# Second mixer: attention pieces written between the channel tiles of the projections, scores in two-bank PSUM pairs

## The chip, the cores and the metric

One core of a Trainium2 chip runs the whole program. The metric is the device time of one execution in microseconds (us). The engines are TensorE (PE, with its weight loads PEld shown apart), VectorE (DVE), ScalarE (ACT), GpSimd (POOL, used here only to issue DMAs and to clear buffers) and SyncE (SP, which issues the weight loads from memory).

## The reference

A two-layer trunk over 384 tokens (256 latent ones, columns 0 to 255, and 128 context ones, columns 256 to 383), model width 1024, all in float32. Each layer is a feed-forward block, a mixer and a second feed-forward block. The change is in the second layer's mixer:

```python
def gqa_mixer(h, w_in, g_q, g_k, w_out, ctx):
    B, S, _ = h.shape
    q, k, v = jnp.split(h @ w_in, [MIX_C, MIX_C + GQA_KV_HEADS * GQA_HEAD_DIM], axis=-1)
    q = rms_norm(q.reshape(B, S, GQA_HEADS, GQA_HEAD_DIM), g_q)
    k = rms_norm(k.reshape(B, S, GQA_KV_HEADS, GQA_HEAD_DIM), g_k)
    ...                                   # rotary positions and 128 cached keys for the latent tokens
    o = block_attention(...)              # softmax(q k * 64 ** -0.5) v, 16 heads of 64, 4 of keys and values
    return o.reshape(B, S, MIX_C) @ w_out, (k, v)
...
x = x + gm * out
```

Latent tokens see 128 cached and 256 latent keys, context tokens their own 128. The first layer's mixer (eight heads, another projection, and a convolution beside it) shares the attention code, and so part of the change.

## The kernel before, in words

Activations are held channels by tokens. Every projection is done in three matmuls per channel tile (`mm3`): weights and activations are split into a high part and a remainder, and lo x hi, hi x lo and hi x hi are summed in PSUM. One "channel tile" k of a unit is the 128 input channels k for two output tiles of 128, so six matmuls of 384 or 386 columns. The activations' parts are `Hh`, `Hl` (mixer input) and `MXh`, `MXl` (attention output, 8 tiles of 128 channels, one for each pair of heads).

`stream` takes a list of steps. For each step it issues the weight splits for this step and the next, then the step before's `post` (what reads its PSUM result), then this step's matmuls. Weights come by DMA on SP's queue into three buffers `raw`. A split writes 1024 columns at a time into one of four pairs of buffers: `whi` by a cast on ACT (L205), and `wlo` either by a subtraction on DVE (L210), or, where a step has `add=True`, by a negated copy on ACT (L207) and a DMA on POOL's queue that adds the raw weights onto it (L208). Only the first mixer uses `add=True`.

The instructions are not run in the order written. A planner goes through them by that order, lets ready ones pass those that wait, and fixes each engine's sequence before the run. At run time each engine keeps to its sequence, so an instruction that is late holds what stands behind it.

The second mixer is `mixer_c`. Its input projection has six units (k and v in 0 and 1, q in 2 to 5), 48 matmuls each. A unit's `post` scales its two tiles, and for q adds the rotary part (L605 to L620, L1103). `head_sums4` sums squares over the head dimension and takes the reciprocal root, for four q tiles at a time; its result multiplies the scores (`sc`, `nsc`, L1113). Attention works by groups of two heads:

- `scores` (L644): three products a head into two PSUM banks a head, so four banks of `pmm`, which has four;
- `softmax` (L659 to L668): maximum on DVE, exponential and its sum on ACT, reciprocal and scaling on DVE, one head after the other;
- `pv`: seven transposes a head (L682, L686), copied to SBUF by ACT (L684) and DVE (L688), then the products with the values (L694), split into `MXh` and `MXl` (L610, L611).

The scores and the softmax of group 0 are written behind unit 4, the scores of group 1 ahead of unit 5, and the rest of group 0 behind it. Then comes the attention of groups 1 to 7, with nothing else written beside it, and then the output projection, four units of 48 matmuls, each with a `post` (`resid`, L464): it adds the gated result to the residual `X` (L467), makes the next block's `Hh` and `Hl` (L397, L399) and sums squares (L409, L410).

PSUM has eight banks: four one-bank buffers for `pmm`, two for `ptr`, two for `pax`.

Of the kernel before, what the change touches and what calls it, by code (L numbers as in the profile page):

```python
# [6 lines left out]
F32 = mybir.dt.float32  # L7
# [26 lines left out]

NLEAD = ND + 1
# [19 lines left out]
SH1, SC1, G1, SHM, SCM, GM, SH2, SC2, G2 = range(9)  # L55
# [4 lines left out]
def pair_col(i, k):  # L60

    return (k // 4 * 8 + i * 4 + k % 4) * P
# [18 lines left out]
class Trunk:  # L81
    def __init__(self, nc, tc, a):
        self.nc, self.tc, self.a = nc, tc, a
        self.mods = {}
        self.early = []
# [365 lines left out]
    def rsqrt(self, out, src, scale, v=None, w=None):  # L451
# [7 lines left out]
        for _ in range(3):  # L459
            ve.tensor_tensor(out=w, in0=out, in1=out, op=ALU.mult)  # L460
            ve.scalar_tensor_tensor(out=w, in0=w, scalar=-0.5, in1=v, op0=ALU.mult, op1=ALU.mult)  # L461
            ve.scalar_tensor_tensor(out=out, in0=w, scalar=1.5, in1=out, op0=ALU.add, op1=ALU.mult)  # L462

    def resid(self, d, ps, gate, nxt):  # L464
        nc = self.nc
        for s0, s1, c in SEG:
            nc.vector.scalar_tensor_tensor(  # L467
                out=self.X[:, d, s0:s1], in0=ps[:, s0:s1], scalar=gate[:, d, c:c + 1],
                in1=self.X[:, d, s0:s1], op0=ALU.mult, op1=ALU.add)
# [151 lines left out]

    def attention(self, heads, pairs, pool=None):

        nc = self.nc
        S = {}
        room = []
# [7 lines left out]
            return room[n // 3][:, n % 3 * 7 * P:(n % 3 + 1) * 7 * P]  # L634

        def scores(hs):
            for h in hs:
                S[h] = (self.ps_mm(), self.ps_mm())
            for dst, c0, cols, q0 in ((0, 0, slice(0, T), 0), (0, T, slice(T, 512), TL), (1, 0, slice(0, T), P)):
                for h in hs:  # L640
                    qT, kT, rows = heads[h][:3]
                    kw = {"tile_position": (rows.start, 0)} if pairs else {}
                    n = cols.stop - cols.start
                    nc.tensor.matmul(S[h][dst][:, c0:c0 + n], lhsT=qT[rows, q0:q0 + P], rhs=kT[rows, cols],  # L644
                                     start=True, stop=True, **kw)

        Pm = {}

        def softmax(hs):

            st = {h: (self.tb("mx", 3, 4), self.tb("sm", 3, 4), scratch(0, h)) for h in hs}
            part = lambda h, i: (S[h][0][:, 0:T], S[h][1][:, 0:T], S[h][0][:, T:512])[i]
            off = (0, T, 2 * T, 7 * P)
            for ids in ((0, 2), (1,)):
                for h in hs:
                    mx, sm, pr = st[h]
                    sc, nsc = heads[h][4], heads[h][5]
                    for i in ids:
                        nc.vector.reduce_max(out=mx[:, i:i + 1], in_=part(h, i), axis=AX.X)  # L659
                    c = slice(ids[0], 3, 2)  # L660
                    nc.vector.tensor_tensor(out=mx[:, c], in0=mx[:, c], in1=nsc[:, c], op=ALU.mult)
                    for i in ids:
                        nc.scalar.activation(pr[:, off[i]:off[i + 1]], part(h, i), AF.Exp, scale=sc[:, i:i + 1],
                                             bias=mx[:, i:i + 1], accum_out=sm[:, i:i + 1])
                    nc.vector.reciprocal(sm[:, c], sm[:, c])
                    for i in ids:
                        p, r = pr[:, off[i]:off[i + 1]], sm[:, i:i + 1]
                        nc.vector.tensor_scalar(out=p, in0=p, scalar1=r, scalar2=None, op0=ALU.mult)  # L668
            for h in hs:
                S.pop(h)  # L670
                Pm[h] = st[h][2]

        def pv(hs, MXh, MXl, ps=None):
            pts = []
            for h in hs:
                pr = Pm.pop(h)
                pt = scratch(1, h).rearrange("p (a b) -> p a b", b=P)
                pts.append(pt)
                ta, tb = (ps or (self.ps_ax if h == hs[1] else self.ps_tr))(), (ps or self.ps_tr)()
                for kt in range(2):  # L680
                    for qb in range(2):
                        nc.tensor.transpose(ta[:, (2 * kt + qb) * P:(2 * kt + qb + 1) * P],  # L682
                                            pr[:, qb * T + kt * P:qb * T + kt * P + P], self.ident)
                nc.scalar.copy(pt[:, 0:4, :], ta.rearrange("p (a b) -> p a b", b=P))  # L684
                for i, o in enumerate((2 * P, T + 2 * P, 2 * T)):
                    nc.tensor.transpose(tb[:, i * P:i * P + P], pr[:, o:o + P], self.ident)  # L686
                copy = nc.vector.tensor_copy if pool else nc.scalar.copy
                copy(pt[:, 4:7, :], tb[:, 0:3 * P].rearrange("p (a b) -> p a b", b=P))  # L688
# [9 lines left out]

        groups = [list(range(i, i + 2)) for i in range(0, len(heads), 2)]

        def first():
            scores(groups[0])
            softmax(groups[0])

        def ahead(i):
            if i + 1 < len(groups):
                scores(groups[i + 1])

        def group(i, MXh, MXl, ps=None):
            pv(groups[i], MXh, MXl, ps)  # L710
            if i + 1 < len(groups):
                softmax(groups[i + 1])
            self.pop_bg(BG2)

        def rest(MXh, MXl, i0=0):
            for i in range(i0, len(groups)):
                ahead(i)
                group(i, MXh, MXl)

        return first, rest, ahead, group  # L720

    def out_steps(self, w, MXh, MXl, gate, nxt):
        steps = []
# [47 lines left out]
    def mixer_a(self, l, nxt):  # L771
        nc, a, tc = self.nc, self.a, self.tc
        with tc.tile_pool(name="ma", bufs=1, reuse_waits="tile") as mp:
# [7 lines left out]
            with tc.tile_pool(name="map", bufs=1, reuse_waits="tile") as pp:  # L781
# [147 lines left out]
                heads = []  # L929
                for h in range(8):  # L930
                    V = lambda kt, h=h: Vt[:, kt, 64 * h:64 * h + 64]
                    heads.append((qT[h], kT[h], slice(0, P), V, rs, nrs, h // 2, h % 2))
                first, rest, _, _ = self.attention(heads, False)
                w = a["wia"]

                def bg(s):
# [71 lines left out]
    def mixer_c(self, l, nxt):  # L1008
        nc, a, tc = self.nc, self.a, self.tc
        with tc.tile_pool(name="mc", bufs=1, reuse_waits="tile") as mp:  # L1010
# [87 lines left out]
            def p_q(i):  # L1098
                def f(ps):
# [8 lines left out]
                    if i % 4 == 3:  # L1108
                        four = qq[-4:]

                        def sums():
                            r = head_sums4(four)
                            nc.vector.tensor_scalar(out=sc[i // 4], in0=r, scalar1=0.125, scalar2=None, op0=ALU.mult)  # L1113
                            nc.vector.tensor_scalar(out=nsc[i // 4], in0=r, scalar1=-0.125, scalar2=None, op0=ALU.mult)
                        (self.mid if i == 3 else self.later).append(sums)
                return f

            posts = [p_k(0), p_k(1), p_v(0), p_v(1)] + [p_q(i) for i in range(8)]
            heads = []
            for i in range(8):  # L1120
                for h in range(2):
                    kv = 2 * (i % 2) + h
                    V = lambda kt, kv=kv: Vt[:, kt, 64 * kv:64 * kv + 64]
                    norms = [x[i // 4][:, 2 * (i % 4) + h:24:8] for x in (sc, nsc)]
                    heads.append((qT[i], kT[i % 2], slice(64 * h, 64 * h + 64), V, *norms, i, h))
            first, rest, ahead, group = self.attention(heads, True, mp)
            steps = []
            for u in range(6):
                steps.append(self.in_unit(a["wic"][u], posts[2 * u:2 * u + 2]))
# [165 lines left out]
```

## Time and profile before

| | |
|---|---|
| Median of 3 runs | 1481.43 us (1478.88 to 1482.4) |
| The profiled execution | 1478.81 us; its span, first to last instruction, 1477.0 us |
| Granted TensorE clock, mean | 0.992 of full speed |
| PE, PEld | 98% and 95% of the span busy |
| DVE, ACT | 80% and 45% |
| Second mixer, unit 4 to the last output matmul | 1075.51 to 1185.09, 109.58 us |

A row of the timeline has the start, the length, the engine, the line of the kernel, the operation, what it writes and reads, how many instructions the row stands for, and in brackets the idle time before it with what ended it. Lengths of neighbouring matmuls overlap, since PE starts one before the last has drained; the step from start to start is what each costs in a row. A group of the page has the number of instructions, the busy time, the mean duration in ns, and the idle time ahead.

### The profile page before, as it was taken

Reading aid. Unit: us, or ns where it says so; the run is one execution under the profiler, and the core shown is the slowest. Engines: PE = TensorE matmul, PEld = TensorE weight load, DVE = VectorE, ACT = ScalarE, POOL = GpSimd, SP = SyncE. Lnnn points to the kernel's source line nnn. Section 1 sums busy time; section 2 is a strip of 40 time slices with the busy share of each in tenths; the row PEclk is TensorE's granted clock in tenths of the full one; section 3 lists DMA queues with packets and bytes.
Section 4 is the critical chain, followed back from the end, with each engine's and each line's share of the span. In section 5 each row is a group of like instructions: output and inputs, shape, how many; then the busy total and the mean of one; then the engine's idle time right before and its main releaser. Section 6 shows DMA issues by size and latency. Waiting matters only on the chain. (4 is left out here: it accounts for less than half of the span.)

```text
span 1477.0 us, 21867 instructions
## 1 busy us (share of the span) xinstructions
PE 1442.5 (98%) x8278; PEld 1397.7 (95%) x8278; DVE 1178.5 (80%) x2515; ACT 665.3 (45%) x1171; POOL 26.0 (2%) x36
## 2 busy tenths in 40 slices
PE   6999999999989999999999999999999999999997
PEld 5999999999869999999999999999975999999997
DVE  6999999949996999999969997544799688555433
ACT  4443343368666433343344334333476544333332
POOL 0000000021100000000000000000000000000000
PEclk8999999999999999999999999999999999999999
DMA  9655657699646566656565663334420264332341
GB/s 365 239 218 213 243 179 265 213 234 222 149 109 165 233 230 226 228 193 240 197 254 200 217 232 113 100 136 145 137 85 30 65 234 158 124 134 88 118 132 49
DMA packets 44633, 262.53 MB, mean 178 GB/s; under 512 B 4944, under 2 KB 6768, under 8 KB 21232
## 3 DMA queue, kind: packets, MB, share of 16 engines
q1 hardware_dynamic: 38160, 245.04, 46.0%
q0 software_dynamic: 4032, 14.16, 5.2%
q10 hardware_dynamic: 2336, 1.94, 0.4%
q8 instruction: 65, 1.06, 0.3%
q14 instruction: 40, 0.33, 0.1%
HBM read 244.98 MB, written 1.98 MB: 167 GB/s over the span
## 5 line engine op out<-in xcount | busy, mean ns | idle before, releaser
L205 ACT CAST whi<-raw 128x1024 fp32r<-128x1024 f32 (+1 forms) x348 | 329.5, 948 | 583.2 <-PE ps_mm L274 508.5
L272 PE MATMUL ps_mm<-Hh,wlo 128*128 128x386 f32 x1568 | 533.2, 341 | 5.7 <-DVE wlo L210 4.1
L273 PE MATMUL ps_mm<-Hl,whi 128*128 128x386 f32 x1568 | 532.4, 340 | 1.1 <-DVE Hl L399 1.1
L274 PE MATMUL ps_mm<-Hh,whi 128*128 128x386 f32 x1568 | 531.1, 339 | 0.0
L210 DVE TENSOR_TENSOR wlo<-raw,whi 128x1024 fp32r<-128x1024 f32 (+1 forms) x320 | 348.3, 1089 | 155.0 <-ACT whi L205 152.5
L272 PEld LDWEIGHTS ps_mm<-Hh,wlo 128*128 128x128 f32 x1568 | 295.8, 189 | 8.4 <-DVE wlo L210 4.4
L273 PEld LDWEIGHTS ps_mm<-Hl,whi 128*128 128x128 f32 x1568 | 296.9, 189 | 2.3 <-DVE Hl L399 1.4
L274 PEld LDWEIGHTS ps_mm<-Hh,whi 128*128 128x128 f32 x1568 | 296.0, 189 | 0.0
L273 PE MATMUL ps_mm<-Gl,whi 128*128 128x384 f32 x704 | 236.8, 336 | 0.0
L272 PE MATMUL ps_mm<-Gh,wlo 128*128 128x384 f32 x704 | 236.7, 336 | 0.0
L274 PE MATMUL ps_mm<-Gh,whi 128*128 128x384 f32 x704 | 236.7, 336 | 0.0
L375 DVE SCALAR_TENSOR_TENSOR junk<-rawm,eb 128x1024 bf16<-128x1024 f32 x130 | 158.2, 1217 | 1.0 <-ACT eb L144 1.0
L375 DVE SCALAR_TENSOR_TENSOR rawm<-rawm,eb 128x1024 f32<-128x1024 f32 x130 | 158.2, 1217 | 0.3
L273 PEld LDWEIGHTS ps_mm<-Gl,whi 128*128 128x128 f32 x704 | 132.0, 188 | 0.0
L272 PEld LDWEIGHTS ps_mm<-Gh,wlo 128*128 128x128 f32 x704 | 132.0, 187 | 0.0
L274 PEld LDWEIGHTS ps_mm<-Gh,whi 128*128 128x128 f32 x704 | 132.0, 187 | 0.0
L526 ACT CAST Gh<-g 128x384 fp32r<-128x384 f32 x88 | 45.1, 512 | 84.8 <-DVE g L523 84.6
L516 ACT ACTIVATE sa<-ta,ba 128x256 f32<-128x256 f32 (+1 forms) x176 | 70.0, 446 | 4.7 <-DVE ta L513 4.6
L893 DVE SCALAR_TENSOR_TENSOR acc<-ub,vec,acc 128x399 f32<-128x399 f32 x120 | 70.3, 626 | 0.4
L523 DVE SCALAR_TENSOR_TENSOR g<-t,bb,sa 128x256 f32<-128x256 f32 (+1 forms) x176 | 65.2, 412 | 0.9 <-ACT sa L516 0.9
L467 DVE SCALAR_TENSOR_TENSOR X<-ps_mm,mod,X 128x256 f32<-128x256 f32 x88 | 32.6, 411 | 39.0 <-PE ps_mm L274 39.0
L527 DVE TENSOR_TENSOR Gl<-g,Gh 128x384 fp32r<-128x384 f32 x88 | 48.7, 554 | 12.2 <-ACT Gh L526 12.2
(269 smaller groups left out, 1292.6 us busy)
## 6 DMA issues: line engine op xcount, KB each, us to landing
raw<-wi SPq DMA_DIRECT2D x86, 1024.0 KB, 4.8
rawm<-wmt SPq DMA_DIRECT2D x64, 1024.0 KB, 4.8
raw<-wo SPq DMA_DIRECT2D x64, 704.0 KB, 4.2
wlo<-raw POOLq DMA_DIRECT2D x24, 512.0 KB, 6.8
raw<-wia SPq DMA_DIRECT2D x7, 1024.0 KB, 9.0
raw<-wm SPq DMA_DIRECT2D x6, 1024.0 KB, 8.7
raw<-wic SPq DMA_DIRECT2D x6, 1024.0 KB, 4.7
raw<-woc SPq DMA_DIRECT2D x4, 1024.0 KB, 4.8
```

The costliest lines, as they stand in the source:

```text
L205: self.nc.scalar.copy(hi, raw)
L210: self.nc.vector.tensor_tensor(out=lo, in0=raw, in1=hi.bitcast(F32), op=ALU.subtract)
L272: mm(out, lhsT=lo, rhs=rh, start=start, stop=False)
L273: mm(out, lhsT=hi, rhs=rl, start=False, stop=False)
L274: mm(out, lhsT=hi, rhs=rh, start=False, stop=stop)
L375: self.nc.vector.scalar_tensor_tensor(out=junk, in0=raw[:, i], scalar=1.0, in1=self.eb[:, c], op0=ALU.mult, op1=ALU.mult, accum_out=out[:, ...
L467: nc.vector.scalar_tensor_tensor(out=self.X[:, d, s0:s1], in0=ps[:, s0:s1], scalar=gate[:, d, c:c + 1], in1=self.X[:, d, s0:s1], op0=ALU.m ...
L516: nc.scalar.activation(sa[:, s0:s1], ta[:, s0:s1], AF.Silu, bias=ba[:, c:c + 1])
L523: nc.vector.scalar_tensor_tensor(out=g[:, s0:s1], in0=t2[:, s0:s1], scalar=bb[:, c:c + 1], in1=sa[:, s0:s1], op0=ALU.add, op1=ALU.mult)
L526: nc.scalar.copy(Gh[:, f], g)
L527: nc.vector.tensor_tensor(out=Gl[:, f], in0=g, in1=Gh[:, f].bitcast(F32), op=ALU.subtract)
L893: nc.vector.scalar_tensor_tensor(out=acc[j], in0=src(t), scalar=w(t), in1=acc[j], op0=ALU.mult, op1=ALU.add)
```

## The change

1. PSUM: `pmm` has two buffers of two banks. `ps_mm` hands out the halves of one in turn; `ps_two` takes a whole one.
2. `scores` puts the same product of both heads into one two-bank tile. `softmax` takes the maxima of both heads in one instruction, and one product and one reciprocal for both; exponentials and scaling stay one for each head. The first mixer's attention gets this too, and keeps its order otherwise.
3. `pv` is cut into `turn` (the transposes and copies of one head, T) and `values` (products and split, V).
4. In `mixer_c` one stream runs units 0 to 3 as before, then units 4 and 5 and eight half units of the output projection by scripts. In a script `c3` is channel tile 3, `S2` the scores of group 2, `M2` its softmax, `T20` and `T21` the transposes of its two heads, `V2` its values, `N0` and `N1` the head sums, and `n4` tile 4 of the next step. The lower half (channel tiles 0 to 3, groups 0 to 3) of all four output units comes first and is added to `X` by `add_to`; the upper half follows, with `resid`. The half units are steps 0 to 7.
5. Units 4 and 5 and the half units split their weights with `add=True`.

```diff
-PB = (4, 2, 2)
+PB = (2, 2, 2)
+MIX_IN = ("c0 c1 N0 S0 M0 c2 c3 c4 c5 S1 M1 T00 c6 T01 c7 V0",
+          "c0 S2 M2 T10 c1 T11 c2 V1 c3 S3 M3 T20 c4 T21 c5 V2 c6 c7")
+MIX_OUT = ("S4 T30 c0 T31 c1 V3 c2 c3 N1 M4", "c0 c1 c2 c3", "S5 M5 T40 c0 T41 c1 V4 c2 c3",
+           "S6 M6 T50 c0 T51 c1 V5 c2 c3", "S7 M7 T60 c4 T61 c5 V6 c6 T70 n4 T71 n5 V7 n6 c7", "c7", "c4 c5 c6 c7",
+           "c4 c5 c6 c7")
...
+    def ps_two(self):
+        return self.pmm.tile([P, 2, 512], F32, tag="mm", name="ps_mm")
+
     def ps_mm(self):
-        return self.pmm.tile([P, 512], F32, tag="mm", name="ps_mm")
+        if self.bank is None:
+            two = self.ps_two()
+            self.bank = two[:, 1]
+            return two[:, 0]
+        one, self.bank = self.bank, None
+        return one
...
+    def add_to(self, d, ps, gate):
+        for s0, s1, c in SEG:
+            self.nc.vector.scalar_tensor_tensor(
+                out=self.X[:, d, s0:s1], in0=ps[:, s0:s1], scalar=gate[:, d, c:c + 1],
+                in1=self.X[:, d, s0:s1], op0=ALU.mult, op1=ALU.add)
...
         def scores(hs):
-            for h in hs:
-                S[h] = (self.ps_mm(), self.ps_mm())
+            S[hs[0]] = st = (self.ps_two(), self.ps_two())
...
         def softmax(hs):
+            part = (S0[:, :, 0:T], S1[:, :, 0:T], S0[:, :, T:512])
             for ids in ((0, 2), (1,)):
-                for h in hs:
...
+                for i in ids:
+                    nc.vector.reduce_max(out=mx[:, i], in_=part[i], axis=AX.X)
+                c = slice(ids[0], 3, 2)
+                nc.vector.tensor_tensor(out=mx[:, c], in0=mx[:, c], in1=nsc[:, c], op=ALU.mult)
+                for j, pr in enumerate(prs):
                     for i in ids:
+                        nc.scalar.activation(pr[:, off[i]:off[i + 1]], part[i][:, j], AF.Exp, scale=sc[:, i, j:j + 1],
+                                             bias=mx[:, i, j:j + 1], accum_out=sm[:, i, j:j + 1])
+                nc.vector.reciprocal(sm[:, c], sm[:, c])
+                for j, pr in enumerate(prs):
+                    for i in ids:
+                        p = pr[:, off[i]:off[i + 1]]
+                        nc.vector.tensor_scalar(out=p, in0=p, scalar1=sm[:, i, j:j + 1], scalar2=None, op0=ALU.mult)
...
+            def in_part(u, script):
+                def mm(s):
+                    st["p"] = [self.ps_tr(), self.ps_tr()]
+                    for o in script.split():
+                        if o[0] != "c":
+                            piece(o)
+                            continue
+                        k = int(o[1])
+                        for i, p in enumerate(st["p"]):
+                            self.mm3(p[:, :TB], *s.w(pair_col(i, k)), self.Hh[:, k], self.Hl[:, k], k == 0, k == ND - 1)
...
+                return Step(a["wic"][u], UN, True, mm, post, add=True)
...
+            def out_part(u, h, script):
+                def chunk(s, k):
+                    if not ps:
+                        get = self.ps_mm if h and u % 2 else self.ps_tr
+                        ps.extend((get(), get()))
+                    for i, p in enumerate(ps):
+                        self.mm3(p[:, :T], *s.w(pair_col(i, k) - h * half), MXh[:, k], MXl[:, k],
+                                 k == 4 * h, k == 4 * h + 3)
...
+                def post():
+                    for i, p in enumerate(ps):
+                        if h:
+                            self.resid(2 * u + i, p, self.mods[l, GM], nxt)
+                        else:
+                            self.add_to(2 * u + i, p, self.mods[l, GM])
+                outs.append(Step(a["woc"][u][:, h * half:h * half + half], half, True, mm, post, add=True))
...
+            steps = [self.in_unit(a["wic"][u], posts[2 * u:2 * u + 2]) for u in range(4)]
+            steps += [in_part(u, x) for u, x in zip((4, 5), MIX_IN)]
+            for i, x in enumerate(MIX_OUT):
+                out_part(i % 4, i // 4, x)
+            self.stream(steps + outs)
-            steps[4] = self.in_unit(a["wic"][4], posts[8:10], self.ps_tr, None, first)
-            steps[5] = self.in_unit(a["wic"][5], posts[10:12], self.ps_tr, lambda: ahead(0),
-                                    lambda: group(0, MXh, MXl, self.ps_ax))
-            self.stream(steps)
-            rest(MXh, MXl, 1)
-            self.stream(self.out_steps(a["woc"], MXh, MXl, lambda: self.mods[l, GM], nxt))
```

More of the change, by code (lines that the diff above doesn't have):

```diff
@@ L84, in __init__ @@
         self.mods = {}
+        self.bank = None
         self.early = []
@@ L462, in rsqrt @@
             ve.scalar_tensor_tensor(out=out, in0=w, scalar=1.5, in1=out, op0=ALU.add, op1=ALU.mult)
+    def add_to(self, d, ps, gate):
[3 more added lines that the diff above has]
+                in1=self.X[:, d, s0:s1], op0=ALU.mult, op1=ALU.add)
     def resid(self, d, ps, gate, nxt):
         nc = self.nc
[L466 to L469, printed above, removed]
+        self.add_to(d, ps, gate)
         if nxt is not None:
@@ L643, in scores @@
                     n = cols.stop - cols.start
-                    nc.tensor.matmul(S[h][dst][:, c0:c0 + n], lhsT=qT[rows, q0:q0 + P], rhs=kT[rows, cols],
+                    nc.tensor.matmul(st[dst][:, i, c0:c0 + n], lhsT=qT[rows, q0:q0 + P], rhs=kT[rows, cols],
                                      start=True, stop=True, **kw)
@@ L649, in softmax @@
         def softmax(hs):
-            st = {h: (self.tb("mx", 3, 4), self.tb("sm", 3, 4), scratch(0, h)) for h in hs}
-            part = lambda h, i: (S[h][0][:, 0:T], S[h][1][:, 0:T], S[h][0][:, T:512])[i]
+            S0, S1 = S.pop(hs[0])
+            mx, sm = (self.tb(t, 6, 4).rearrange("p (t h) -> p t h", h=2) for t in ("mx", "sm"))
+            prs = [scratch(0, h) for h in hs]
+            part = (S0[:, :, 0:T], S1[:, :, 0:T], S0[:, :, T:512])
             off = (0, T, 2 * T, 7 * P)
+            sc, nsc = heads[hs[0]][4:6]
@@ L662, in softmax @@
+                nc.vector.reciprocal(sm[:, c], sm[:, c])
+                for j, pr in enumerate(prs):
                     for i in ids:
[L663 to L688, printed above, removed]
+                        p = pr[:, off[i]:off[i + 1]]
@@ L689, in pv, with values @@
+        def values(hs, pts, MXh, MXl):
             o = self.ps_ax()
@@ L699, in attention @@
         groups = [list(range(i, i + 2)) for i in range(0, len(heads), 2)]
+        if pool:
+            return groups, scores, softmax, turn, values
         def first():
@@ L703, in first, with rest @@
             softmax(groups[0])
[L705 to L720, printed above, removed]
+        def rest(MXh, MXl):
+            for i, hs in enumerate(groups):
+                if i + 1 < len(groups):
+                    scores(groups[i + 1])
+                pts = []
+                for h in hs:
+                    turn(h, self.ps_ax if h == hs[1] else self.ps_tr, self.ps_tr, pts)
+                values(hs, pts, MXh, MXl)
+                if i + 1 < len(groups):
+                    softmax(groups[i + 1])
+                self.pop_bg(BG2)
+        return first, rest
     def out_steps(self, w, MXh, MXl, gate, nxt):
@@ L931, in mixer_a @@
                     V = lambda kt, h=h: Vt[:, kt, 64 * h:64 * h + 64]
-                    heads.append((qT[h], kT[h], slice(0, P), V, rs, nrs, h // 2, h % 2))
-                first, rest, _, _ = self.attention(heads, False)
+                    both = [x.unsqueeze(2).to_broadcast([P, 3, 2]) for x in (rs, nrs)]
+                    heads.append((qT[h], kT[h], slice(0, P), V, *both, h // 2))
+                first, rest = self.attention(heads, False)
                 w = a["wia"]
@@ L1107, in f, with sums @@
                     qq.append(sq)
[L1108 to L1115, printed above, removed]
-                return f
+                return f
+            def sums(j):
+                r = head_sums4(qq[4 * j:4 * j + 4])
+                nc.vector.tensor_scalar(out=sc[j], in0=r, scalar1=0.125, scalar2=None, op0=ALU.mult)
+                nc.vector.tensor_scalar(out=nsc[j], in0=r, scalar1=-0.125, scalar2=None, op0=ALU.mult)
             posts = [p_k(0), p_k(1), p_v(0), p_v(1)] + [p_q(i) for i in range(8)]
@@ L1123, in mixer_c @@
                     V = lambda kt, kv=kv: Vt[:, kt, 64 * kv:64 * kv + 64]
[L1124 to L1129, printed above, removed]
-            steps[4] = self.in_unit(a["wic"][4], posts[8:10], self.ps_tr, None, first)
@@ new lines, in mixer_c, with piece @@
+            groups, scores, softmax, turn, values = self.attention(heads, True, mp)
+            pts = {}
+            def piece(o):
+                i = int(o[1])
+                if o[0] == "S":
+                    scores(groups[i])
+                elif o[0] == "M":
+                    softmax(groups[i])
+                elif o[0] == "T":
+                    turn(groups[i][int(o[2])], self.ps_ax, self.ps_ax, pts.setdefault(i, []))
+                elif o[0] == "V":
+                    values(groups[i], pts.pop(i), MXh, MXl)
+                else:
+                    sums(i)
@@ new lines, in mixer_c @@
+            half = UN // 2
+            def in_part(u, script):
+                st = {}
+                def mm(s):
[8 more added lines that the diff above has]
+                def post():
+                    for f, p in zip(posts[2 * u:2 * u + 2], st["p"]):
+                        f(p)
+                return Step(a["wic"][u], UN, True, mm, post, add=True)
```

40 lines of the change are left out of this document (34 added, 6 removed).

## The prediction

> **What bounds the kernel now.** I read the page's busy table first, then the windows over the second mixer, then TensorE's timeline there, and last what its instructions wait for.
>
> ```profile
> PE 1442.5 (98%) x8278; PEld 1397.7 (95%) x8278; DVE 1178.5 (80%) x2515; ACT 665.3 (45%) x1171; POOL 26.0 (2%) x36
> ...
> 1075.51:1084.20 8.69, 8.69 (x54) 7.71 (x54) 7.14 (x21) 5.50 (x11) 0.00 (x0) 1.00 0.31 121
> 1084.20:1100.07 15.87, 14.68 (x80) 11.93 (x79) 15.21 (x59) 13.16 (x37) 0.00 (x0) 1.00 0.19 68
> 1100.07:1153.78 53.71, 51.92 (x336) 32.69 (x334) 48.15 (x185) 38.62 (x112) 0.00 (x0) 1.00 0.06 21
> 1153.78:1185.09 31.31, 31.31 (x182) 31.31 (x181) 19.92 (x38) 14.51 (x26) 0.00 (x0) 1.00 0.35 126
> 1075.51:1185.09 109.58, 106.61 (x647) 83.64 (x647) 90.41 (x301) 71.79 (x185) 0.00 (x0) 1.00 0.18 65
> ```
>
> TensorE (PE) is the bound: 98% busy over the span. The window rows have PE, PEld, DVE, ACT, POOL, granted clock, DMA share, GB/s; they are units 4 and 5 of the input projection (two rows), the bare attention stretch, the output projection, and all of it. In the bare attention stretch PE shows 51.92 of 53.71 us as busy, but its weight loads only 32.69, against 31.31 of 31.31 where dense tiles run. So "busy" hides something there. The timeline shows what:
>
> ```profile
> 1085.38 1.78 PE L644 MATMUL ps_mm<-kT,qT 64*128 64x384 f32 x12
> 1087.10 0.44 PE L272 MATMUL ps_tr<-Hh,wlo 128*128 128x386 f32 x1
> 1087.38 0.34 PE L273 MATMUL ps_tr<-Hl,whi 128*128 128x386 f32 x1
> ...
> 1092.06 1.13 PE L644 MATMUL ps_mm<-kT,qT 64*128 64x384 f32 x4 [1.19 <-ACT pr L663]
> ...
> 1093.67 1.78 PE L644 MATMUL ps_mm<-kT,qT 64*128 64x384 f32 x8
> ...
> 1100.07 0.60 PE L682 MATMUL ps_ax<-cst,pr 128*128 128x128 f32 x4
> ...
> 1103.75 1.73 PE L694 MATMUL ps_ax<-pr,Vt 128*64 128x256 f32 x16
> ...
> 1143.81 0.66 PE L682 MATMUL ps_tr<-cst,pr 128*128 128x128 f32 x4
> ...
> 1144.63 0.60 PE L682 MATMUL ps_ax<-cst,pr 128*128 128x128 f32 x4
> ...
> 1145.68 2.39 PE L694 MATMUL ps_ax<-pr,Vt 128*64 128x256 f32 x16
> ...
> PEld ps_mm L644 <- ACT pr L663: 2.9, 10, 0.6
> PEld ps_tr L686 <- ACT pr L684: 2.1, 6, 0.6
> ```
>
> Undisturbed, the 12 score instructions of a pair of heads take 1.78 us (1085.38). In group 1 they come in bits (4, then 8, with a wait of 1.19 us in front) as exponentials free one PSUM bank after another; the totals below say the same of the others. The value products take 1.73 us where both heads are ready together and 2.39 where they are not. So the stretch is a ring of PE, DVE and ACT that wait for each other. The same window by line:
>
> ```profile
> 1075.51:1185.09 109.58, 22.07 (x96) 10.96 (x96) 1.00 0.18 65
> 1075.51:1185.09 109.58, 16.70 (x128) 1.00 0.18 65
> ```
>
> The scores (first row, L644) hold PE for 22.07 us where 8 x 1.78 = 14.2 would do; the value products (L694) for 16.70 where 8 x 1.73 = 13.8 would.
>
> **The change part by part.** The window ends at 1185.09, when the last output matmul hands over to the next feed-forward block. I work out PE's time after the change for the same work, then what it must still wait.
>
> ```profile
> 1075.51 0.34 PE L272 MATMUL ps_tr<-Hh,wlo 128*128 128x386 f32 x1
> 1080.62 0.34 PE L274 MATMUL ps_tr<-Hh,whi 128*128 128x386 f32 x1
> 1080.89 0.85 PE L1046 MATMUL ps_ax<-sqq,cst 128*32 128x384 f32 x8
> 1082.48 0.49 PE L1052 MATMUL ps_ax<-cst,g 128*128 128x128 f32 x3
> ...
> 1184.05 0.34 PE L272 MATMUL ps_mm<-MXh,wlo 128*128 128x384 f32 x1
> 1184.92 0.34 PE L274 MATMUL ps_mm<-MXh,whi 128*128 128x384 f32 x1
> ```
>
> 1. Channel tiles (the c's). 29 matmul steps from 1075.51 to 1080.62 are 0.176 us each, 5 steps from 1184.05 to 1184.92 are 0.174. 96 x 0.176 + 192 x 0.174 = 50.3 us. Splitting the output units in halves adds no matmul.
> 2. Scores S: 8 x 1.78 = 14.2. With a pair of heads in one two-bank tile, both heads' products of a bank pair become free at once, so the pairs no longer fall apart.
> 3. Transposes T: one head takes 0.82 us (1143.81 to 1144.63); 16 x 0.82 = 13.1.
> 4. Value products V: a c lies ahead of each, so both heads are ready: 8 x 1.73 = 13.8.
> 5. Head sums N: 2 x (0.85 + 0.49) = 2.7.
> 6. Going back and forth. After the scores the first tile steps 0.28 us (1087.10 to 1087.38) instead of 0.176, and I charge the way in the same 0.1. The scripts hold about 26 stretches of pieces between c's: 26 x 0.2 = 5.2.
>
> Sum 99.3 us against 109.58: at most 10.3 us to gain here.
>
> What PE must still wait. Each piece stands in PE's queue, so if it is late, the c's behind it wait too. That is new. The nearest row of before is unit 5, which already had S1 written into it: from 1087.10 to the first transpose at 1100.07 is 12.97 us for 48 x 0.176 + 1.78 + 0.2 = 10.4, so 2.55 us lost with one group. The other end is nothing. What decides is whether a softmax M fits under the PE work that the scripts put between one S and the next:
>
> ```profile
> 1078.89 0.52 ACT L1103 ACTIVATE sqq<-qb 128x384 f32<-128x384 f32 x1
> ...
> 1085.40 0.18 DVE L1113 TENSOR_SCALAR sc<-r 128x24 f32<-128x24 f32 x1
> ...
> 1094.86 0.54 DVE L659 TENSOR_REDUCE mx<-ps_mm 128x1 f32<-128x384 f32 x1
> ...
> 1099.82 0.68 ACT L663 ACTIVATE pr<-ps_mm,mx,sc 128x384 f32<-128x384 f32 x1
> ...
> 1101.55 0.41 DVE L668 TENSOR_SCALAR pr<-pr,sm 128x384 f32<-128x384 f32 x1
> ```
>
> M1 of before held its banks from 1094.86 to 1100.50, 5.6 us, and was done at 1101.96, 7.1 us. The new order has, between S5 and S6, two T, V and four c (1.64 + 1.73 + 4 x 1.05 = 7.6 us), and in unit 5 three c (6.5 us). Both cover 5.6, and T of the group comes after the next S, at 8.3 us or more, which covers 7.1. It does not fit in two places. Between S0 and S1 there are only four c, 4.2 us. And N0, written after c1, needs squares that come 3.9 us into unit 4 (1078.89 + 0.52 - 1075.51), and its scale took from 1080.89 to 1085.40, 4.5 us more; M0 has to wait for it. c6 and c7 can be moved up there, as the planner moved tiles of unit 5 ahead of S1 before. N1 and M4 repeat this with the four c of step 1 as cover, whose two PSUM banks must first be read by step 0's additions. I take 5 us in all (0.6 a group), nearer to nothing than to 2.55, because of the 7.6 against 5.6.
>
> The other engines' share:
>
> ```profile
> L210 DVE TENSOR_TENSOR wlo<-raw,whi 128x1024 fp32r<-128x1024 f32 x12 | 14.7, 1222 | 6.0 <-ACT whi L205 6.0
> L659 DVE TENSOR_REDUCE mx<-ps_mm 128x1 f32<-128x128 f32 x16 | 4.5, 280 | 0.0
> L207 ACT ACTIVATE wlo<-raw 128x1024 fp32r<-128x1024 f32 (+1 forms) x28 | 28.7, 1030 | 23.4 <-PE ps_mm L272 20.6 <-PE ps_tr L272 2.7
> wlo<-raw POOLq DMA_DIRECT2D x24, 512.0 KB, 6.8
> 1184.77 1.39 DVE L467 SCALAR_TENSOR_TENSOR X<-ps_mm,mod,X 128x256 f32<-128x256 f32 x4 [1.33 <-PE ps_mm L274]
> 1187.52 0.74 DVE L399 SCALAR_TENSOR_TENSOR Hl<-X,mod,Hh 128x256 fp32r<-128x256 f32 x2
> 1188.18 0.55 DVE L410 TENSOR_TENSOR ssq<-ssq,sq 128x384 f32<-128x384 f32 x1
> ```
>
> 7. Weight splits of units 4, 5 and the output halves go from DVE to ACT and to accumulating DMAs on POOL's queue: 12 x 1.22 us off DVE, 12 x 1.03 onto ACT, 12 DMAs that land in 6.8 us. A low half is then ready 1.05 + 1.03 + 6.8 = 8.9 us after its start. The buffers (four halves) let it start when the half four places before is used up, which lies a unit or more ahead, so I charge nothing; without that cover step 2, behind the short step 1 of 4.2 us, would wait some 5 us, once. SP's loads become eight of half the size, on a queue at 0.18 DMA share.
> 8. Eight `add_to` put 8 x 0.7 = 5.6 us on DVE (1.39 us is two channels). Two maxima in one instruction lie between one reduction (0.55) and two (1.10); from 0.55 at 384 and 0.28 at 128 elements I take 0.95. With fewer products and reciprocals DVE saves about 0.5 us a group. The exponentials of the first head start up to 0.8 us later, under the cover above. ACT's window is then 71.8 + 12.4 = 84 of some 104 us, DVE below 80: neither becomes the bound.
> 9. The end. Pairs of channels are finished every 8.3 us now, each with 1.39 + 2 x 0.74 + 2 x 0.55 = 4.0 us on DVE. In the new order steps 5, 6, 7 last 1.05, 4.2 and 4.2 us, so three pairs (12 us) meet 9.4 us, and the last Hl comes some 6.5 us into the next block, whose k = 6 tile is due after 36 x 0.176 = 6.3. Price 0 to 4, I take 0.5.
> 10. The first mixer gets the paired softmax too, with conv taps filling DVE:
>
> ```profile
> 420.00:430.00 10.00, 6.46 (x40) 4.19 (x39) 9.59 (x28) 5.05 (x16) 0.00 (x0) 1.00 0.29 105
> ```
>
> DVE is full there (9.59 of 10), so 4 groups x 0.5 us saved come through, less the later first exponential: -1.5, between -3 and +2. In the feed-forward blocks a PSUM pair is the two tiles of one input step, freed together anyway, or two neighbouring output channels, of which the next pair has the other tile: nothing.
>
> Sum: -10.3 + 5 + 0.5 - 1.5 = -6.3 us. The profiled execution took 1478.81 us (span 1477.0), the median run 1481.43, 2.6 more. So 1472.5 by the profile, 1475 on the median's scale.
>
> **The rivals.**
>
> (B) The waits eat the gain: about 1.3 us a group instead of 0.6. Then -10.3 + 10.4 - 1.0 = -0.9: 1480.5. For it: unit 5's 2.55 and the two places that don't fit. Against it: 7.6 against 5.6 us elsewhere.
>
> (C) On the other side: late pieces at the head of PE's queue hold the tiles behind them in every group as in unit 5 of before. Place: units 4 and 5 and output steps 0 to 4. Price 8 x 2.55 = 20.4, so -10.3 + 20.4 - 1.0 = +9.1: 1490.5. It makes the kernel slower from 1.4 us a group on. Against it: of unit 5's loss, the 1.19 us wait was for banks freed singly.
>
> (F) The two banks of a pair are held together: a matmul into the second half waits for the reader of the first. Then each odd channel of a feed-forward output waits for its neighbour's residual:
>
> ```profile
> 1395.25 0.74 DVE L467 SCALAR_TENSOR_TENSOR X<-ps_mm,mod,X 128x256 f32<-128x256 f32 x2 [0.75 <-PE ps_mm L274]
> ```
>
> About 0.8 us, 4 times in each of 4 blocks: +13, 1488. Nothing in the trace speaks for it; the banks are separate.
>
> (E) PE's true load is its weight loads. The window has 83.64 us of them, so 109.58 - 83.64 = 26 us could go: 1455.5. Against it: an undisturbed score instruction loads weights for a fraction of its time, so the share can't come to one there. The Trainium skill, "Perfetto Trace Analysis", section "Identifying the Most-Contended Engine", holds matmul occupancy to be a poor measure of closeness to the roofline and takes weight-load busy time in its place; the trace agrees that occupancy misleads (97% in the bare stretch), not that all the rest is free.
>
> **How the numbers follow.** Forecast 0.56 (own range 1468 to 1477), B 0.25, C 0.10, F 0.06, E 0.03. A measurement of this kernel can tell about 0.3% (4.4 us) from no change. Faster by more: forecast and E, 0.59; within: B, 0.25; slower: C and F, 0.16. The range takes the forecast with its bounds (all 10.3 gained and 3 in the first mixer: 1468, and 2 more for the back-and-forth charge) and B up to its far end: 1466 to 1486. It leaves out C, F and E, 0.19.
>
> **What the profile after would show.** Right: the scores in one piece of 12 at about 1.8 us, no bare attention stretch, window from unit 4 to the next block about 104 us, L207 up by 12 and L210 down by 12. Wrong: PE waits before L644 or L682 of over 1 us a group (B, C), waits before odd channels in feed-forward outputs (F), a hole of over 2 us at the start of the next block (9), or waits of PE for the accumulated low halves (7).

## The result, and the profile after

The changed kernel takes 1516.81 us (median of 5 runs, 1516.02 to 1520.45), the kernel before 1478.88 us on the same chip: a ratio of 1.0257, 95% interval 1.0244 to 1.027. It is slower by 38 us; the forecast was 1475, in a range of 1466 to 1486. The profiled execution has a span of 1514.2 us against 1477.0.

The busy row of the page after the change (the row of before stands at the head of the prediction):

```profile
PE 1449.0 (96%) x8278; PEld 1395.7 (92%) x8278; DVE 1167.8 (77%) x2435; ACT 676.7 (45%) x1183; POOL 36.5 (2%) x48
```

The windows over the four feed-forward output stretches (columns PE, PEld, DVE, ACT, POOL, granted clock, DMA share, GB/s), first before, with two of the four rows left out, then after:

```profile
218.67:310.89 92.22, 92.22 (x529) 92.22 (x529) 80.21 (x148) 38.35 (x61) 2.72 (x3) 1.00 0.69 231
...
945.16:1037.39 92.23, 92.23 (x530) 92.23 (x530) 44.20 (x73) 34.90 (x57) 0.00 (x0) 1.00 0.40 136
```

```profile
218.16:322.02 103.86, 96.04 (x530) 94.77 (x529) 80.35 (x148) 38.86 (x61) 2.73 (x3) 0.97 0.62 205
678.62:779.68 101.06, 95.00 (x529) 93.74 (x529) 79.97 (x144) 35.48 (x57) 0.00 (x0) 0.98 0.57 197
966.59:1063.18 96.59, 93.25 (x529) 91.99 (x529) 44.65 (x74) 34.83 (x57) 0.00 (x0) 1.00 0.39 130
1405.26:1501.71 96.45, 94.38 (x542) 93.37 (x542) 36.28 (x56) 31.03 (x46) 0.00 (x0) 1.00 0.27 90
```

PE has the same 8278 instructions. The four stretches, which the change was not aimed at, took 92.22 us each and now take 103.86, 101.06, 96.59 and 96.45: 29.1 us more. The waits of the changed kernel (us in total, times, longest) and its timeline tell why:

```profile
PE ps_mm L289 <- DVE X L483: 19.3, 15, 2.5
...
PE ps_mm L289 <- DVE wlo L227: 8.7, 2, 5.1
```

```profile
254.93 1.22 DVE L392 SCALAR_TENSOR_TENSOR rawm<-rawm,eb 128x1024 f32<-128x1024 f32 x1
...
256.07 0.82 DVE L227 TENSOR_TENSOR wlo<-raw,whi 128x640 fp32r<-128x640 f32 x1
256.81 0.74 DVE L483 SCALAR_TENSOR_TENSOR X<-ps_mm,mod,X 128x256 f32<-128x256 f32 x2
...
257.60 0.44 PE L289 MATMUL ps_mm<-Gh,wlo 128*128 128x384 f32 x1 [2.52 <-DVE X L483]
...
978.31 0.74 DVE L483 SCALAR_TENSOR_TENSOR X<-ps_mm,mod,X 128x256 f32<-128x256 f32 x2 [0.74 <-PE ps_mm L291]
...
979.11 0.44 PE L289 MATMUL ps_mm<-Gh,wlo 128*128 128x384 f32 x1 [0.83 <-DVE X L483]
```

The first matmul of channels 1, 3, 5 and 7 of every block (15 of the 16 are recorded as waits) starts when the residual of its even neighbour (L483) has read PSUM. PE is idle for 0.6 to 0.84 us where DVE is free. In the first two blocks five of the eight waits are 2 to 2.5 us, because the residual stands in DVE's queue behind the sums of the modulation weights (L392) and the splits (L227).

The second loss is at the end of the mixer:

```profile
1199.77 1.39 DVE L483 SCALAR_TENSOR_TENSOR X<-ps_tr,mod,X 128x256 f32<-128x256 f32 x4 [0.71 <-PE ps_tr L291]
...
1212.91 0.48 DVE L416 SCALAR_TENSOR_TENSOR Hl<-X,mod,Hh 128x256 fp32r<-128x256 f32 x1
1213.31 1.22 DVE L227 TENSOR_TENSOR wlo<-raw,whi 128x1024 fp32r<-128x1024 f32 x1
...
1214.67 0.66 PE L289 MATMUL ps_mm<-Hh,wlo 128*128 128x386 f32 x1 [5.06 <-DVE wlo L227]
```

From 1199.77 on DVE does residuals almost without a pause, and the subtraction that splits the next block's first weights (L227) stands behind most of them. PE is idle for 5.06 us. The input stretch behind it takes 3.7 us more than before (190.6 against 186.9, from its first matmul to the first of the output): 1.4 of it are nine matmuls at a lower clock right behind the hole, 2.3 another wait for DVE, at 1235.86.

The window that the change was aimed at, unit 4 to the last output matmul, fell from 109.58 to 108.11 us. Its scores alone (PE, PEld) take 18.34 us, where they took 22.07:

```profile
1101.34:1209.45 108.11, 18.34 (x96) 8.61 (x96) 1.00 0.50 137
```

So the parts are +29.1 in the feed-forward outputs, +5.1 for the hole, +3.7 behind it, -1.5 in the window and +1.5 in the first mixer. Together they make 37.9; the spans differ by 37.2. The first mixer's 1.5 tells nothing: with paired scores it took between 167.5 and 172.4 us in the profiled executions below, with one-bank scores 168.2 (before) and 167.7 to 171.5.

### The profile page after: what moved, and what is told of

Its sections match the earlier page's. It is cut to its first block, busy times and chain, and to the rows that moved or that the text cites. A ratio compares the mean times of both kernels' runs of the same rounds, so it can differ in the third digit from the quotient of the medians.

```text
span 1514.2 us, 21769 instructions
## 1 busy us (share of the span) xinstructions
PE 1449.0 (96%) x8278; PEld 1395.7 (92%) x8278; DVE 1167.8 (77%) x2435; ACT 676.7 (45%) x1183; POOL 36.5 (2%) x48
## 5 line engine op out<-in xcount | busy, mean ns | idle before, releaser
L227 DVE TENSOR_TENSOR wlo<-raw,whi 128x1024 fp32r<-128x1024 f32 (+2 forms) x308 | 333.6, 1085 | 160.4 <-ACT whi L222 158.1
L289 PE MATMUL ps_mm<-Gh,wlo 128*128 128x384 f32 x704 | 240.3, 341 | 19.3 <-DVE X L483 19.3
L392 DVE SCALAR_TENSOR_TENSOR rawm<-rawm,eb 128x1024 f32<-128x1024 f32 x130 | 158.6, 1220 | 0.6
L392 DVE SCALAR_TENSOR_TENSOR junk<-rawm,eb 128x1024 bf16<-128x1024 f32 x130 | 158.5, 1219 | 0.4 <-ACT eb L161 0.4
L536 ACT ACTIVATE sa<-ta,ba 128x256 f32<-128x256 f32 (+1 forms) x176 | 70.5, 448 | 30.2 <-DVE ta L533 30.1
L225 POOL DMA_DIRECT2D wlo<-raw x40 | 34.7, 870 | 1147.5 <-ACT wlo L224 1122.6
L483 DVE SCALAR_TENSOR_TENSOR X<-ps_mm,mod,X 128x256 f32<-128x256 f32 x84 | 31.6, 412 | 37.9 <-PE ps_mm L291 37.9
```

Of the source, the lines that this page charges most:

```text
L225: self.nc.gpsimd.dma_start(out=lo.bitcast(F32), in_=raw, accum_op=ALU.add)
L227: self.nc.vector.tensor_tensor(out=lo, in0=raw, in1=hi.bitcast(F32), op=ALU.subtract)
L289: mm(out, lhsT=lo, rhs=rh, start=start, stop=False)
L392: self.nc.vector.scalar_tensor_tensor(out=junk, in0=raw[:, i], scalar=1.0, in1=self.eb[:, c], op0=ALU.mult, op1=ALU.mult, accum_out=out[:, ...
L483: self.nc.vector.scalar_tensor_tensor(out=self.X[:, d, s0:s1], in0=ps[:, s0:s1], scalar=gate[:, d, c:c + 1], in1=self.X[:, d, s0:s1], op0= ...
L536: nc.scalar.activation(sa[:, s0:s1], ta[:, s0:s1], AF.Silu, bias=ba[:, c:c + 1])
```

## The experiments

The kernel before ran beside each experiment; its medians were 1478.1 to 1480.25 us.

### The feed-forward outputs: experiments 1, 2 and 12

1, on the changed kernel:
```diff
-                        st["p"] = self.ps_mm()
+                        st["p"] = self.ps_tr() if d % 2 else self.ps_two()[:, 0]
```


> The changed kernel, but in the feed-forward outputs each channel has a PSUM buffer of its own (even channels the first bank of a pair, odd channels a one-bank buffer). Theory F (the two banks of a pair are held together, so an odd channel's first matmul waits for its neighbour's residual): the four output stretches go back from 104.0, 101.2, 96.8 and 96.6 us to 92.4 each, and the time falls by 29 us, 1516.8 to about 1488 (1485 to 1490). Rival (the stretches are long because the granted clock dips and DVE has a worse order there, whatever the PSUM): they stay within 2 us of what they are, 1513 to 1517.

2, on the kernel before: only `PB` and `ps_mm` as in the change.

> The kernel before, with one thing changed: its four one-bank buffers are handed out as halves of two two-bank buffers; no order is changed, no paired softmax, no scripts. Theory F: the feed-forward outputs alone lose 25 to 30 us, so 1504 to 1510; the old attention, which takes four halves a group, may lose some more, up to 8 us. Rival (the loss needs the new order or the new softmax): 1479, within 3 us.

12, on the changed kernel:
```diff
-                        st["p"] = self.ps_mm()
+                        if d % 4 == 0:
+                            two = self.ps_two(), self.ps_two()
+                            self.four = [two[i % 2][:, i // 2] for i in range(4)]
+                        st["p"] = self.four[d % 4]
```


> The changed kernel, but neighbouring channels of a feed-forward output get halves of different two-bank buffers (channels 0 and 2 share one, 1 and 3 the other); all buffers stay shared. Theory F (an odd channel's first matmul waits for the residual that reads the other half of its own buffer): the reader is then a channel earlier and done, so the same gain as with buffers of their own, 1487 to 1492. Rival (sharing itself costs, reads of one bank of a pair while TensorE writes the other): 1510 to 1517.

Measured: 1 takes 1489.47 us, 27.3 less than the changed kernel; 2 takes 1525.4, 45 more than the kernel before beside it (1480.25); 12 takes 1488.05. The first output stretch in 12, and the waits of all of 2:

```profile
217.59:309.82 92.23, 92.23 (x530) 92.23 (x530) 79.88 (x148) 38.91 (x61) 2.72 (x3) 1.00 0.69 231
```

```profile
PE ps_mm L278 <- DVE X L473: 19.1, 15, 2.4
```

Theory F holds. Handing out halves is enough to bring the same 15 waits into the kernel before. There the outputs lost 31 us; 2 lost more than expected, since its two mixers also became 8 us longer each (probably because the old attention takes four halves a group; no run separates that). And 12 shows what the halves are held by: they stay shared, but with the neighbour in another buffer the reader of the other half is a channel earlier and done, and the whole loss is gone. So having two users in a buffer costs nothing by itself. In 12 no half is read while the other is written, so 12 alone says nothing on that; but the rows of the changed kernel show no such overlap either. PE stands idle, and the matmul starts at 979.11, when the two residual instructions that began at 978.31 have run their 0.74 us.

### The hole: experiment 3

```diff
-                step = Step(wi[f], UN, True, lambda s: upto(s, ND), post)
+                step = Step(wi[f], UN, True, lambda s: upto(s, ND), post, add=(l, which) == (1, 1) and f < 1)
```


> The first experiment's kernel, and the first input unit of the last feed-forward block gets its low half by the copy on ACT and the accumulating DMA, so it no longer stands behind the residuals in DVE's queue. Theory (the hole of 5.06 us at the end of the mixer, and the slow 3.7 us after it, come from this one subtraction): 5 to 8.5 us less than the first experiment, so 1479 to 1483. Rival (the backlog of residuals itself sets it, the last Hl being ready only at the same moment): the hole moves by a few matmuls, at most 2 us less, 1485 to 1488.

1479.97 us, 9.5 less than experiment 1 (whose input stretch, 193.5 us, was longer than the 190.6 of the changed kernel): the hole is gone, and 1.6 us remain in the input stretch. With F and the hole removed the change stands at 0.9997 of the kernel before (0.9984 to 1.0011): no difference.

### Pairs, interleaving, weight splits: experiments 4, 5 and 6

4: experiment 1 with the order of before in `mixer_c` (units 4 and 5, bare attention, whole output units, subtractions on DVE).

> The first experiment's kernel with the order of before in the second mixer (units 4 and 5, then the bare attention, then whole output units, subtractions on DVE): paired scores and paired softmax alone. Theory of the prediction's steps 2 and 4 (the pairs by themselves put the scores in one piece, 22.1 us to 14.2): 5 to 9 us less than before, 1470 to 1474. Rival (what PE saves on scores it then waits for in the bare stretch, since the ring of maximum, exponential, scaling and copies sets its length): 1477 to 1482. Second rival (the first head's exponential waits for both heads' maximum, so each group gets longer): 1483 to 1488.

5: experiment 3 without `add=True` in units 4, 5 and the output halves.

> The third experiment's kernel, with the weight splits of units 4 and 5 and of the eight output halves back on DVE (a subtraction of 1.22 us each, 12 of them) in place of the copy on ACT and the accumulating DMA. Theory (step 7: both ways lie under other work, DVE having room in this window): 1480, within 2 us of the third experiment. Rival (DVE has no room: 14.7 us more on it delay the maxima and the residuals): 1484 to 1492. Second rival (the accumulating DMA lands late for some units, 0.4 and 0.85 us at two unit starts): 1478.

6: the scripts, with `PB = (4, 2, 2)`, one-bank scores and the old softmax (and the split of experiment 3).

> The scripts without the pairs: four one-bank buffers as before, each head its own two banks and its own softmax, the feed-forward outputs as before, and the first feed-forward input unit of the last block split as in the third experiment. Theory P (the 9.7 us that the pairs cost in the old order come from the bare stretch, where the softmax is exposed; between channel tiles it is covered): the second mixer takes 146 us as in the third experiment, 1478 to 1481. Rival Q (the pair's later first exponential and later release cost between the tiles too): 4 to 8 us less, 1472 to 1476. Rival R (banks freed singly cut the scores into bits, as in the kernel before): 2 to 5 us more, 1482 to 1485.

| | median us | unit 4 to the next block's first matmul |
|---|---|---|
| before | 1478.88 | 109.6 |
| 3: scripts, pairs | 1479.97 | 108.1 |
| 4: old order, pairs | 1488.49 | 119.2 |
| 5: scripts, pairs, splits on DVE | 1479.28 | 109.6 |
| 6: scripts, one bank | 1479.47 | 108.7 |

In the old order the pairs alone cost 9.7 us in this window, against my theory and a little past what the second rival allowed. The waits of the attention stretch of experiment 4:

```profile
PE ps_mm L665 <- ACT pr L685: 9.1, 9, 2.1
PE ps_mm L289 <- ACT pr L685: 1.9, 1, 1.9
```

Before, the same wait (scores for the exponentials that free their banks) was 0.5 us. One-bank buffers let the next scores start on the first head's banks while the second head's exponentials ran; a pair is free only after both. So in the bare stretch the bits into which the scores fell were a gain, not a loss. Experiment 4 changes the buffers and the softmax together; which of the two costs more is not shown. Written between channel tiles, in the planner's order, the pairs neither gain nor lose (6 against 3), and neither does the way of the splits (5): those two theories hold. The interleaving is worth 11.1 us only against the pairs in bare order; against the kernel before it brought 1.5 in this window, and nothing in the whole time.

### What a change between kinds of instruction costs: experiments 9 and 10

On the kernel before, with unused transposes in one output block (9 as shown, 10 with the line in the comment):
```diff
+                        for i in {2: (0,), 4: (1,), 6: (2,), 8: (3,)}.get(k, ()):      # experiment 10: {5: (0, 1, 2, 3)}
+                            nc.tensor.transpose(extra[:, i * P:i * P + P], self.cst[:, K_ID:K_ID + P], self.ident)
```


> The kernel before, with 64 transposes of a constant (128 by 128, unused) added in the outputs of the third feed-forward block, each one by itself between matmuls, four in every 11 channel tiles: 128 changes between the two kinds of instruction. Theory (a change costs about 0.095 us each way, the first channel tile behind a piece stepping 0.27 us in place of 0.176): the stretch grows by 64 x (0.11 + 0.19) = 19 us, 92.1 to about 111. Rival (the changes are free and the time goes to waits): 64 x 0.11 = 7 us, 99.

> The same 64 transposes, four together in each half channel: 32 changes. Theory: 16 x (4 x 0.11 + 0.19) = 10 us, 102, so 9 us less than with single ones. Rival: the same as with single ones, 99.

The stretch of 92.06 us (first to last matmul) became 99.63 with 64 single transposes and 99.33 with 16 groups of four: 0.118 us a transpose alone, 0.114 in a group. My theory of 0.095 us a change is refuted for transposes. The tile behind a single transpose does step 0.26 us at first, but the transpose itself steps only 0.03 (950.82 to 950.85 in experiment 9). For scores, values and head sums no run prices a change alone.

### Why the window is 108 us: experiments 7, 8, 11, 13, 14 and 15

The prediction's sum said 104.3 (99.3 of work, 5 of waits). The rows of the changed kernel show scores, values and head sums taken apart by the planner:

```profile
1103.55 0.84 PE L1070 MATMUL ps_ax<-sqq,cst 128*32 128x384 f32 x4
1104.32 0.91 PE L665 MATMUL ps_mm<-kT,qT 64*128 64x384 f32 x2
1105.16 0.83 PE L1070 MATMUL ps_ax<-sqq,cst 128*32 128x384 f32 x2
...
1132.63 0.65 PE L717 MATMUL ps_ax<-pr,Vt 128*64 128x256 f32 x2
1133.20 1.91 PE L665 MATMUL ps_mm<-kT,qT 64*128 64x384 f32 x10
1135.05 1.73 PE L717 MATMUL ps_ax<-pr,Vt 128*64 128x256 f32 x14
...
1155.30 0.85 PE L1070 MATMUL ps_ax<-sqq,cst 128*32 128x384 f32 x8
```

Two or four head sums take as long as eight (0.76 and 0.77 us to the next start, 0.78 for all), two value instructions 0.57 and the other fourteen still 1.65. Scores took 18.2 us by starts where I had put 14.2, values 15.6 for 13.8, head sums 3.8 for 2.7: 6.9 over. Tiles and transposes with all changes and waits took 70.5 where I had 73.6.

All of these are made from experiment 3, with new scripts and with each head sum cut in two pieces, N and O. 7 and 8: TensorE's sequence fixed to the scripts (each instruction ordered behind the one written before it), units in the order k, q, q, v, q, q, T behind S; 8 with one bank.

> The third experiment's kernel with TensorE's sequence in this part fixed to the order written, the units taken in the order k, q, q, v, q, q, and scripts that put T behind S and leave one to two channel tiles between T and V; about 45 changes between kinds of instruction in place of 88. Theory (each change costs about 0.1 us, and each group's softmax has 9 us of other work behind its scores): 4 us less for the changes and 2 to 4 less for waits, 1471 to 1476. Rival (a fixed order makes TensorE wait where the planner had let tiles pass, so the cuts were the cheaper way): 1481 to 1492.

> The same fixed order with one-bank scores and one softmax a head, as in the scripts-without-pairs experiment. Theory P: the same as the fixed order with pairs, within 2 us, 1471 to 1476. Rival Q (pairs cost between tiles too): 4 to 8 us below the fixed order with pairs. Rival R: 2 to 5 us above it.

11: as 7, `T00 c T01 c V`.

> The fixed order again, with a channel tile between the two heads' transposes and another ahead of the values, so that the copies of PSUM lie under it. Theory (the loss of the first fixed order was the 5.3, 3.5 and 2.5 us of waits for copies; the changes cost 0.1 us each and there are some 64 in place of 88): the second mixer takes 142 to 145 us where the third experiment took 146.3, so 1476 to 1479. Rival (a fixed order can't let tiles pass late pieces, and waits return elsewhere): 1481 to 1488.

13: S, V, N, O whole, tiles and transposes free between them. 14: `"S2 M2 T10 c3 T11 c4 V1"` becomes `"S2 T10 c3 T11 M2 c4 V1"`, and so in all groups but 0 and 4.

> The third experiment's kernel with scores, values and head sums each kept whole in TensorE's sequence (nothing may pass into or across such a piece; channel tiles and transposes between two of them may still pass each other), the scripts being put in the order that the planner had given them. Theory (cuts: two score instructions alone take 0.84 us where twelve in one piece take 1.71, two value instructions alone 0.57 with the other fourteen still 1.66, two head sums alone 0.76 where eight take 0.78, so the cuts of the third experiment's kernel cost 4.0 + 2.3 + 1.1 us): scores 14.2 us, values 13.4, head sums 2.6, and the second mixer 146.3 - 5 to 7 = 139 to 142, 1473 to 1476. Rival (the cuts filled time that was idle anyway, waiting for the copies and exponentials on ACT): scores and values as the theory says, but as much again in new waits ahead of values and transposes, 146 or more, 1480 or more.

> The same, and each group's softmax is written behind the transposes of the group before, so that their copies come ahead of its exponentials on ACT. Theory (in the fixed orders the values waited 2.1 us a group because their copies stood behind exponentials in ACT's queue): where the run before has waits of values for ACT, they fall below 0.5 us a group; the softmax ends 2 to 3 us later, which 8.4 us between two scores leave room for; 0 to 5 us less than the run before. Rival (the later softmax comes out on the path, TensorE waiting in front of transposes and scores): 3 to 10 us more than the run before.

15, on 14:
```diff
-"c0 c1 N0 S0 O0 M0 c2 c3 ...", "... S3 T20 c5 T21 M3 c6 V2 c7", "c0 S4 T30 c1 T31 N1 c2 V3 O1 M4 c3"
+"c0 c1 c2 N0 S0 O0 M0 c3 ...", "... S3 T20 c5 T21 M3 c6 c7 V2", "S4 T30 c0 T31 c1 N1 c2 V3 O1 M4 c3"
```


> The run before (pieces whole, copies first) with two pieces moved to where its trace had TensorE waiting: the first head sums behind channel tile 2 instead of 1 (they took 3.09 us there, 0.78 undisturbed), and the last values of unit 5 behind its last channel tile with the scores of group 4 at the head of the next step (2.64 us of wait for unit 5's results there). Theory (the remaining loss against the prediction's sum is a few such places, each its own wait): 3 to 5 us less than the run before, second mixer 143 to 145 us, 1475 to 1478. Rival (the ring of scores, softmax and copies sets the length, and a wait removed in one place comes back in the next): 147 us again, 1480 to 1482.

| | median us | second mixer, first unit to the next block |
|---|---|---|
| before / 3 | 1478.88 / 1479.97 | 147.7 / 146.3 |
| 7, 8, 11: fixed order | 1488.87, 1501.17, 1489.16 | 156.2, 169.3, 157.3 |
| 13: pieces whole | 1488.15 | 154.1 |
| 14: copies first | 1480.83 | 147.6 |
| 15: two pieces moved | 1475.36 | 144.0 |

The fixed orders took 10 us and more above what the theory allowed: 7 lies within its rival's range, 11 just past it, and 8 beyond all three of its own. In this order the pairs did matter: 8, with one bank, takes 12.3 us more than 7. There PE waits 10.3 us ahead of transposes for DVE's copies, in four places; in 7 it waits 2.5 us for them. So it is for the planner's order alone that the pairs are shown to make no difference. Experiment 13 came out as its rival said: scores 14.4 us and nothing between the head sums (the first eight still came as 4, 2 and 2, the later ones waiting for their squares), but as much again in waits. The waits of PE in this window, for 13, 14 and 15:

```profile
PE ps_ax L722 <- ACT pr L710: 7.8, 5, 1.8
PE ps_tr L294 <- PE ps_tr L296: 1.3, 3, 0.6
```

```profile
PE ps_tr L294 <- DVE ta L630: 2.6, 1, 2.6
...
PE ps_ax L722 <- ACT pr L710: 0.2, 1, 0.2
```

```profile
PE ps_mm L670 <- ACT pr L690: 2.0, 3, 1.7
PE ps_ax L708 <- DVE pr L714: 1.4, 2, 0.7
```

In 13 the values (L722) wait for the copies of the transposes (L710), which stand in ACT's queue behind the next group's exponentials (L690):

```profile
1107.02 0.68 ACT L690 ACTIVATE pr<-ps_mm,mx,sc 128x384 f32<-128x384 f32 x1
...
1107.66 0.60 ACT L710 COPY pr<-ps_ax 128x512 f32<-128x512 f32 x1
...
1108.32 1.73 PE L722 MATMUL ps_ax<-pr,Vt 128*64 128x256 f32 x14 [1.76 <-ACT pr L710]
```

The planner's cuts had filled this time. With the copies written first the wait falls from 7.8 to 0.2 us; the two largest places left, moved in 15, give 3.6 us more. The window from unit 4 is then 105.8 us, near the sum. Experiment 15 is the fastest version: 0.9983 of the kernel before (0.9973 to 0.9994), so 2.5 to 3 us, less than the 0.3% that I had called the limit.

## Why the prediction was wrong

Step 10 failed, in its last sentence: "or two neighbouring output channels, of which the next pair has the other tile: nothing". The pair of channels that matters is the one inside a tile. The price was in the text as rival F, with a chance of 0.06 and the ground that "the banks are separate"; that says nothing of how the program orders a writer of one half against a reader of the other. F was also mis-sized, 13 us for 29: 15 recorded waits have 19.3 us of idle, since five of them are 2.0 to 2.5 us and not 0.8 (the residual finds no free DVE there); each of the 16 costs some 0.3 us more, 4.8 (the last matmul ahead of it runs 0.34 us where the step is 0.175, and the first behind it steps 0.28); and three are followed by a stretch at half clock (below), 4.7. Together 28.8 of the 29.1 us. The prediction had named waits before odd channels and a hole of over 2 us as signs of being wrong, and both came.

Step 9 put 0.5 us at the end, 0 to 4. It followed the residuals to the last Hl, some 6.5 us into the next block; that Hl came 5.3 us behind the window's end, so this was nearly right. What it left out is the rest of DVE's queue: the next block's first split, due at once. The hole and what followed it cost 8.8 us.

Steps 2, 4 and 5 took each piece as one, which in the planner's order it is not: 6.9 us. Step 2's reading of the rows of before was wrong in kind too: in experiment 4, where the pairs stand in the old order, the wait for exponentials rose from 0.5 to 9.1 us, so the bits had been overlap. The rest of the window came out 3.1 us below the sum: by starts, and without waits, the channel tiles took 56.3 us where steps 1 and 6 had 55.5, the transposes 11.6 for 13.1, and the waits beside them 2.5 for the 5 charged. So the window missed by 3.8 us. Its 8.8 us above the 99.3 of work are near rival B's 10.4, but by another way: all waits of PE in it come to 3.1 us, and the rest is cut pieces and changes. Had only this failed, the time would have been 1479, inside the range.

Step 7 and the 1.5 us of the first mixer in step 10: the splits are hidden (experiment 5); the first mixer shows no gain.

## What to carry to other kernels

When buffers are merged, list every user of the pool and ask for each whether a writer of one part now follows a reader of the other; handing out neighbours from different buffers is enough. Before work is put at the end of a stage, list all that the next stage needs from that engine's queue, splits of weights as well as activations. And pieces that are laid between other work need their copies ahead of the next exponentials in ACT's queue before it pays to keep them whole.

## What was not expected of the hardware

A wait of TensorE can cost twice. The windows of the changed kernel behind the wait that ended at 257.60 (PE busy, granted clock, DMA share, GB/s), and at the end of the hole:

```profile
257.50:259.00 1.50, 1.40 (x7) 0.82 0.76 306
259.00:261.00 2.00, 2.00 (x8) 0.50 0.99 413
261.00:263.00 2.00, 2.00 (x11) 0.78 0.49 206
263.00:265.00 2.00, 2.00 (x14) 1.00 0.00 0
...
1214.60:1216.00 1.40, 1.33 (x4) 0.50 0.00 0
1216.00:1218.00 2.00, 2.00 (x8) 0.60 0.26 41
```

In the outputs, 0.6 to 1.2 us after the restart, matmuls step 0.32 us instead of 0.176 for some 3.3 us, ten of them; behind the hole they do so at once. In the outputs this followed waits of 1.99, 2.38 and 2.52 us, but not two of 2.08 and 2.40, and none of 0.84 or less. The windows that begin ahead of the waits of 2.40 and 1.99 us:

```profile
716.00:722.00 6.00, 5.15 (x29) 1.00 0.68 210
742.00:748.00 6.00, 5.58 (x23) 0.72 0.39 123
```

The length of the wait does not decide alone: behind a wait of 2.05 us in the last block's input the clock stayed at 1.00 in the changed kernel and was 0.57 over the next 4 us in experiment 1. The Trainium skill, "TensorE: Matmul & The Clock Gate", section "Part 1: The HAM clock gate", has the clock fall after an idle window of about 3.4 us; here a wait of 1.99 us was enough, and one of 2.40 was not.

The Trainium skill, "TensorE: Matmul & The Clock Gate", section "Part 3: Packing small matmuls — row/col tiling", says that products in different tiles of the array run at the same time. That two head sums (0.76 us) take as long as eight (0.78) agrees with it. The trace adds the other side: work that is cut out of such a group is not cheaper by its share.
